# Two places for the normalised probabilities, and two cast operands that change slots, in a hybrid attention and pooling layer

## The chip, the cores and the metric

The kernel runs on one core of a Trainium2 chip. The metric is the device time of one execution in microseconds (us), the median over several runs; less is better.

The core's engines work in parallel, each through its own queue in order: PE multiplies matrices (PEld loads its weights), DVE and POOL work elementwise, ACT does the same and the functions (exp, sigmoid, square), SP issues the DMAs. They wait for each other by semaphores. PE writes its results into PSUM banks; everything else here lies in SBUF.

## The reference

x is 4096 tokens of 1024 channels, float32. One layer:

```python
h = rmsnorm(x, pre_norm_g)
q, k, v, g_a, u_p, g_p = split(h @ w_in)          # 512, 128, 128, 512, 512, 512 columns
# attention: 8 query heads, 2 key/value heads of 64; |i - j| <= 128, blocks of 128 queries
s = where(valid, q @ k.T * scale + bias, -1e30)
m = maximum(max(s), sink)
p = exp(s - m) / (sum(exp(s - m)) + exp(sink - m))
a = (p @ v) * silu(g_a)
# pooling: centred means over 2, 4, 8, 16 tokens minus the token, a linear map, a scale
b = multiscale_pool(u_p, pool_w, pool_scale) * silu(g_p)
x = x + rmsnorm(concat([a, b]) @ w_out, post_norm_g)
```

## The kernel before

Float32 accuracy comes from pairs of float16 numbers: a value is split into a high part (a cast) and a low part (the value minus its cast), and a product is three float16 matmuls. A first phase makes the weights and, for all tokens, the gates g_a and the gated pooling result, which go to DRAM (`ga_scr`, `yp_scr`). It ends at about 555 us of the profile and the change doesn't touch it.

The second phase goes through the 32 blocks of 128 queries from block 31 down to block 0; one block is one slot. Blocks 2u and 2u + 1 form pair u (16 pairs). Each slot has two *halves* of four heads each; a half b, half goes through these steps:

- `scores` (PE, L650), `logits` (DVE, four custom instructions, L671: bias, mask and minimum), `exps` (ACT, L682, four; the sink enters by a column that POOL copies into the tile p, L665), `denominators` (DVE, L689 and L692: `den`, `rd`);
- `probs` (ACT, L704, four): p times rd as float16 into the first half of the tile `pn`; `rests` (DVE, L712, four): the low part into the second half of `pn`;
- `turn` (SP, L721): one transposing DMA from `pn` to `pt`; then `values` (PE, L792) for both halves of a block, and `gate` (DVE, L800).

`pn` has one place (`PN_BUFS = 1`), so the `probs` of a half wait until the transposing DMA of the half before has read it.

The output projection of a pair takes seven products instead of eight, by sums of its four quarters (Strassen's scheme in Winograd's form). Its left operands are y11 and y12, y22, and the four sums s1 to s4. Here a11 is the gated attention of block 2u + 1, a21 that of block 2u, and a12 and a22 are the pooling results of the two blocks, which `pool_in` loads (tiles yf1, yf0). Each operand is cast by `high` (ACT, L809) and completed by `low` (POOL, L813); `pair(t, u, name, f)` enters both. `sum1`, `sum3`, `sum2` (DVE, L842 to L848) and `sum4` (POOL, L851) form the sums. `product` (PE, L873) runs 12 matmuls; in the profile the products of y11, y12 and y22 write `m`, those of s1 to s4 write `ms`. `add` and `gain11` (DVE, L905, L893), `begin` and `square` (ACT, L883, L888), `gain` (POOL, L900), `mean` (DVE L915, POOL L920: `rs`), `residual` (DVE, L924) and `store` finish the pair in the tiles `mo`.

The product of s4 (`mix_p3`) is summed by PE onto the bank in which the product of s1 (`mix_p5`) lies, but one `add` needs the product of s1 alone; so s4 waits for this `add`.

In the steady part PE's order is, in an even slot: scores of half 0, the first q projection, values of the odd block above, scores of half 1, the second q projection, s3 (`mix_p7`), s1 (`mix_p5`). In the next odd slot: scores of half 0, s4 (`mix_p3`), the k and v projections, values of the even block above, scores of half 1, y11, y22, y12, s2 (`mix_p1`, `mix_p4`, `mix_p2`, `mix_p6`).

What sets the order on each engine is a list of due times: `due(t, fn, ...)` enters a call, `now[0]` is the planned time of PE, t0 its value at the start of a slot, and at the end the list is run in order of t. These times are a plan only; on the chip each engine runs its rows in the order that results, each as soon as its waits allow.

Of the kernel before, what the change touches and what calls it, by code (L numbers as in the profile page):

```python
# [9 lines left out]
F16 = mybir.dt.float16  # L10
# [7 lines left out]
P = 128  # L18
# [5 lines left out]
NB = S // P  # L24
BPM = T // P
NH = 8
PT_BUFS = 3
PN_BUFS = 1
EPS = 1e-6
NEG = -1e30  # L30

# [33 lines left out]
def hybrid_layer(ctx: ExitStack, tc, io, out):  # L65
# [76 lines left out]
    with ExitStack() as actx:  # L142
# [387 lines left out]
        for m in range(NM):  # L530
# [5 lines left out]
            for j in range(4):  # L536
                u = pa.tile([P, T + 16], F32, name=f"u{m}_{j}", tag="u", bufs=6)
# [44 lines left out]
    pb = ctx.enter_context(tc.tile_pool(name="pb", bufs=2, reuse_waits="tile"))  # L582
# [19 lines left out]
    def split(dst_h, dst_l, acc):  # L602
        nc.scalar.mul(dst_h, acc, QKV_EVAC)
        nc.vector.scalar_tensor_tensor(
            out=dst_l, in0=acc, scalar=QKV_EVAC, in1=dst_h, op0=ALU.mult, op1=ALU.subtract
        )
# [22 lines left out]
    def due(t, fn, *args):  # L629
        plan.append((t, len(plan), fn, args))  # L630
# [67 lines left out]
    def probs(b, half, i):  # L698
        nk = len(keys(b)) * P
        if i == 0:  # L700
            pn_t[b, half] = pb.tile(
                [P, 2 * 4 * 3 * P], F16, name=f"pn{b}_{half}", tag="pn", bufs=PN_BUFS
            )
# [52 lines left out]
        split(k_all[:, 0, ts], k_all[:, 1, ts], kv_t[u][:, 0])  # L756

    def keep_v(u):
        v = pb.tile([P, 2, 2, P], F16, name=f"vv{u}", tag="v", bufs=4)
        split(v[:, 0], v[:, 1], kv_t.pop(u)[:, 1].rearrange("p (b d) -> p b d", b=2))  # L760
        v_t[u] = v

# [41 lines left out]
    at, yf, y_t, mo_t, z_t, ss_t, xr_t, rs_t = {}, {}, {}, {}, {}, {}, {}, {}  # L804

    def high(u, name, f):

        y_t[u, name] = pb.tile([P, 4, 2, P], F16, name=f"y{name}_{u}", tag=f"y{name}", bufs=1)
        nc.scalar.copy(y_t[u, name][:, :, 0], f(u))  # L809

    def low(u, name, f):
# [3 lines left out]
    def pair(t, u, name, f):  # L815
        due(t, high, u, name, f)
        due(t + 0.65, low, u, name, f)
# [35 lines left out]
    def sums(u, t):  # L853
        due(t, sum1, u)
        due(t + 0.05, sum3, u)
        due(t + 0.1, sum2, u)
        pair(t + 1.4, u, "s2", a11)
        pair(t + (10.0 if u > 1 else 2.0 + 2.0 * u), u, "s3", a21)
        pair(t + (10.6 if u > 1 else 2.6 + 2.0 * u), u, "s1", a_s1)
        due(t + 5.0, sum4, u)  # L860
        pair(t + (11.3 if u > 1 else 7.0), u, "s4", a12)

    LO, HI = slice(0, 512), slice(512, D)
# [76 lines left out]
    now = [0.0]  # L940
    dummy = pb1.tile([P, 1], F32, name="dummy")

    def pe(us, fn, *args):

        due(now[0], fn, *args)
        now[0] += us
        return now[0]
# [4 lines left out]
    def visit(b, half):  # L952
        now[0] = max(now[0], free[0])
        t = max(pe(1.1, scores, b, half), free[1])
        softmax(b, half, t)
        free[:] = t + 2.9, t + 7.9

    def do_kv(u, i=2, late=0.0):
        pe(2.6, proj_k, u, i)
        t = pe(2.8, proj_v, u)  # L960
        due(t + late, keep_k, u)
        due(t + late + 0.5, keep_v, u)

    def do_q(u, half, late=0.0):
        due(pe(5.3, proj_q, u, half) - half + late, keep_q, u, half)

    def attend(b):
        t = pe(2.1, values, b)
        due(t, gate, b)
        if b % 2:  # L970
            pair(t + 0.8, b // 2, "11", a11)
        else:
            sums(b // 2, t + 0.7)
# [3 lines left out]
    def mix_p1(u):  # L977
        due(pe(M, product, u, "11", O11, 0) - 2.0, begin, u)

    def mix_p4(u):  # L980
        pe(M, product, u, "22", OT4, 2)

    def mix_p2(u):
        t = pe(M, product, u, "12", O21, 0, True)
        due(t, square, u, 0, 0, 0)
        due(t + 0.1, gain11, u)

    def mix_p6(u):
        due(pe(M, product, u, "s2", OT2, 1), add, u, (0, HI), (0, HI), 1)

    def mix_p7(u):
        t = pe(M, product, u, "s3", OT3, 0)
        due(t - 1.5, add, u, (1, HI), (0, HI), 0)
        due(t - 1.4, add, u, (1, LO), (1, HI), 2)
        due(t + 1.4, square, u, 1, 0)
        due(t + 2.0, gain, u, 1, LO)

    def mix_p5(u):
        t = pe(M, product, u, "s1", OT1, 1)
        due(t, add, u, (1, HI), (1, HI), 1)  # L1000
        due(t + 0.7, square, u, 1, 1)
        due(t + 1.4, gain, u, 1, HI)
        finish(u, 1, t + (1.5 if u == 0 else 4.0))

    def mix_p3(u):
        t = pe(M, product, u, "s4", O22, 1, True)
        due(t, add, u, (0, HI), (0, HI), 1)
        due(t + 0.7, square, u, 0, 1)
        due(t + 1.4, gain, u, 0, HI)
        finish(u, 0, t + (1.5 if u == 0 else 4.0))  # L1010

    def finish(u, i, t):

        due(t, mean, u, i)
        for n, cs in enumerate((LO, HI) if u == 0 else (slice(0, D),)):
            due(t + 2.0 + 0.7 * n, residual, u, i, cs)
            due(t + 3.4 + 0.7 * n, store, u, i, cs)
# [3 lines left out]
    u = NU - 1  # L1021
# [10 lines left out]
    for b in reversed(range(NB)):  # L1032
        u = b // 2
        t0 = now[0]
        due(t0 + 10.0, load_ga, b)
        if b % 2 == 0 and 0 < b < NB - 2:
            due(t0 + 9.0, load_xr, u + 1, 1)
            due(t0 + 9.0, load_xr, u + 1, 0)
        if b > 0:
            visit(b, 0)  # L1040
        if b == NB - 1:
            do_q(u, 1, 2.8)
            due(now[0] + 0.1, load_x, u - 2)
            now[0] += 2.5
            visit(b, 1)
            do_kv(u - 1, 2, 2.5)
            now[0] += 3.0
        elif b == NB - 3:
            due(free[1], load_wo, OT3)
            mix_p4(u + 1)  # L1050
            mix_p1(u + 1)
            attend(b + 1)
            visit(b, 1)
            due(free[1], load_wo, OT1)
            due(free[1] + 8.0, load_wo, O22)
            do_kv(u - 1, 1)
            mix_p2(u + 1)
            mix_p6(u + 1)
        elif b == 1:
            mix_p3(u + 2)  # L1060
            mix_p4(u + 1)
            visit(b, 1)
            attend(b + 1)
            mix_p1(u + 1)
            mix_p2(u + 1)
            visit(b - 1, 0)
            mix_p6(u + 1)
        elif b % 2:
            mix_p3(u + 2)
            do_kv(u - 1)  # L1070
            attend(b + 1)
            visit(b, 1)
            mix_p1(u + 1)
            mix_p4(u + 1)
            mix_p2(u + 1)
            mix_p6(u + 1)
        elif b:
            do_q(u - 1, 0, 2.0 * (b == NB - 2))
            if b < NB - 2:
                attend(b + 1)  # L1080
            visit(b, 1)
            do_q(u - 1, 1, 2.0 * (b == NB - 2))
            due(now[0] + 2.1, load_x, u - 3)
            if b == NB - 2:
                attend(b + 1)
            else:
                mix_p7(u + 1)
                mix_p5(u + 1)
        else:
            due(t0, load_xr, 1, 1)  # L1090
            due(t0, load_xr, 1, 0)
            mix_p7(1)
            visit(b, 1)
            mix_p5(1)
            attend(1)
            mix_p3(1)
            mix_p4(0)
            mix_p1(0)
            attend(0)
            due(now[0] + 1.0, load_xr, 0, 1)  # L1100
            due(now[0] + 1.0, load_xr, 0, 0)
            mix_p2(0)
            now[0] += 3.0
            mix_p6(0)
            mix_p7(0)
            mix_p5(0)
            mix_p3(0)
        if b % 2 and b < NB - 1:
            due(now[0] - 1.0, pool_in, u, 0)
            due(now[0] + 2.0, pool_in, u, 1)  # L1110
        elif b % 2 == 0:
            t = t0 + 8.6 + 5.0 * (b == NB - 2)
            pair(t, u, "22", a22)
            pair(t + 0.4, u, "12", a12)
    E = mybir.EngineType
    with tc.manual_schedule(engines={E.PE, E.DVE, E.Activation, E.Pool, E.SP}):
        for t, n, fn, args in sorted(plan, key=lambda s: s[:2]):
# [73 lines left out]
```

## Time and profile before

| | us |
|---|---|
| median of 3 runs (lowest, highest) | 1285.51 (1284.38, 1286.82) |
| the profiled execution | 1288.93 |
| its span in the profile | 1287.2 |
| PE busy, in all | 1214.8 |
| DVE busy | 823.8 |
| ACT busy | 637.3 |
| POOL busy | 344.9 |

The span is the time from the first instruction to the last; the profiled execution took 1.7 us more. Busy time is that in which an engine works on an instruction; waiting is not busy. In the rows of the trace a name stands without its number, so `pn` is any half's tile; in the order of instructions below, pn16_1 is the tile of block 16, half 1, and y22_8 the operand y22 of pair 8 (the number behind the last underscore only tells tiles apart).

### The profile page before, as it was taken

How to read it: one execution, taken by the hardware profiler on the slowest of the kernel's cores; microseconds unless marked ns; L12 is line 12 of the kernel's file. 1: busy time of each engine (PE TensorE's matmuls, PEld its weight loads, DVE VectorE, ACT ScalarE, POOL GpSimd, SP SyncE). 2: the span in 40 equal slices, each digit the busy share in tenths (PEclk: the TensorE clock that was granted, in tenths of full speed). 3: DMA queues.
4: the chain of work that ended last, by engine and by line, in shares of the span. 5: the costliest groups of instructions: out<-in, count | busy, mean ns of one | idle time of the engine just before them, and what ended most of it. 6: DMA issues, size and time to landing. Idle time of an engine off the chain costs nothing. (4 is left out here: it accounts for less than half of the span.)

```text
span 1287.2 us, 22201 instructions
## 1 busy us (share of the span) xinstructions
PE 1214.8 (94%) x8630; PEld 703.9 (55%) x8632; DVE 823.8 (64%) x1717; ACT 637.3 (50%) x1352; POOL 344.9 (27%) x356
## 2 busy tenths in 40 slices
PE   5998999999999989989999999999999999999975
PEld 3643444444444434466675766666666757665632
DVE  4576263717155744436777777877787777778774
ACT  5365241512164521135755666566556656666651
POOL 2022020201020101101343333343334433333442
PEclk9998999999999999999999999999999999999998
DMA  7659485827159731275957765776676577656663
GB/s 228 229 144 286 161 207 154 244 92 229 33 173 272 225 106 42 63 232 124 274 118 189 186 169 140 188 181 137 183 187 167 116 184 193 169 136 156 148 147 115
DMA packets 337754, 216.49 MB, mean 168 GB/s; under 512 B 266944, under 2 KB 308544, under 8 KB 334064
## 3 DMA queue, kind: packets, MB, share of 16 engines
q1 hardware_dynamic: 337648, 215.07, 62.3%
q8 instruction: 67, 1.10, 0.4%
q14 instruction: 39, 0.32, 0.1%
HBM read 93.38 MB, written 56.13 MB: 116 GB/s over the span
## 5 line engine op out<-in xcount | busy, mean ns | idle before, releaser
L132 PEld LDWEIGHTS <-wa_h 128*128 128x128 f16 x1520 | 149.3, 98 | 186.2 <-issue 10.1
L712 DVE SCALAR_TENSOR_TENSOR pn<-p,rd,pn 128x384 f16<-128x384 f32 (+1 forms) x256 | 166.5, 696 | 55.3 <-ACT pn L704 55.1
L873 PE MATMUL ms<-wo,ys 128*128 128x512 f16 x768 | 173.9, 379 | 23.3 <-DVE mo L905 19.6
L682 ACT ACTIVATE p<-p,nm 128x385 f32<-128x385 f32 (+1 forms) x256 | 153.1, 600 | 60.5 <-POOL p L665 43.6
L614 PE MATMUL aq<-xt,wb_h 128*128 128x256 f16 x1024 | 174.7, 274 | 0.0
L704 ACT ACTIVATE pn<-p,rd 128x384 f16<-128x384 f32 (+1 forms) x256 | 136.9, 597 | 67.1 <-DMA pt<-pn 44.4
L132 PE MATMUL u<-xt,wa_h 128*128 128x512 f16 x512 | 155.7, 382 | 6.1 <-DVE xp L181 5.5
L671 DVE CUSTOM_DVE_ANT_0 p<-s,bias,nsink 128x384 f32<-128x384 f32 (+1 forms) x256 | 156.0, 663 | 1.0 <-PE s L650 1.0
L132 PE MATMUL ga<-xt,wa_h 128*128 128x512 f16 x512 | 153.6, 379 | 0.0
L132 PE MATMUL gp<-xt,wa_h 128*128 128x512 f16 x496 | 150.3, 382 | 3.3 <-DVE s_gp L432 3.3
L614 PE MATMUL aq<-xt,wb_l 128*128 128x256 f16 x512 | 140.3, 274 | 0.0
L614 PEld LDWEIGHTS <-wb_h 128*128 128x128 f16 x1280 | 125.7, 98 | 25.5 <-issue 9.4
L873 PEld LDWEIGHTS <-ys 128*128 128x128 f16 x768 | 74.5, 98 | 112.4 <-issue 25.4
L873 PE MATMUL m<-wo,y 128*128 128x512 f16 x576 | 129.8, 383 | 1.7 <-POOL y L813 0.9
L132 PEld LDWEIGHTS <-wa_l 128*128 128x128 f16 x760 | 74.7, 98 | 94.0 <-issue 6.1
L900 POOL TENSOR_TENSOR mo<-mo,gpost 128x512 f32<-128x512 f32 x45 | 73.6, 1636 | 119.1 <-ACT jkb L888 117.7
L132 PE MATMUL u<-xt,wa_l 128*128 128x512 f16 x256 | 97.8, 382 | 0.1
L132 PE MATMUL ga<-xt,wa_l 128*128 128x512 f16 x256 | 97.0, 379 | 0.1
L464 POOL TENSOR_TENSOR yt<-yt,s_gp 128x512 f32<-128x512 f32 x32 | 46.6, 1456 | 185.9 <-DVE yt L460 86.6
L873 PEld LDWEIGHTS <-y 128*128 128x128 f16 x576 | 55.2, 98 | 72.2 <-issue 7.6
L132 PE MATMUL gp<-xt,wa_l 128*128 128x512 f16 x248 | 94.7, 382 | 0.0
L432 DVE SCALAR_TENSOR_TENSOR s_ga<-ga,s_ga 128x512 f32<-128x512 f32 x32 | 22.1, 689 | 93.9 <-ACT s_ga L431 93.9
(135 smaller groups left out, 1764.7 us busy)
## 6 DMA issues: line engine op xcount, KB each, us to landing
xn<-in_x SPq DMA_DIRECT2D x32, 512.0 KB, 6.0
xr<-in_x SPq DMA_DIRECT2D x32, 512.0 KB, 4.2
out<-xr SPq DMA_DIRECT2D x30, 512.0 KB, 3.8
x_scr<-xt SPq DMA_DIRECT2D x7, 2048.0 KB, 10.3
xt<-x_scr SPq DMA_DIRECT2D x14, 1024.0 KB, 7.3
ga_scr<-s_ga SPq DMA_DIRECT2D x32, 256.0 KB, 2.3
yp_scr<-yt SPq DMA_DIRECT2D x32, 256.0 KB, 2.7
yf<-yp_scr SPq DMA_DIRECT2D x32, 256.0 KB, 2.8
```

What stands on the lines that cost most here:

```text
L132: mm = nc.tensor.matmul(a3, w[:, k, :], x[:, :, kk, :], start=(n == 0), stop=(n == 3 * KT - 1))
L432: nc.vector.scalar_tensor_tensor(out=s, in0=acc, scalar=scale, in1=s, op0=ALU.mult, op1=ALU.mult)
L464: nc.gpsimd.tensor_tensor(out=t, in0=t, in1=sg, op=ALU.mult)
L614: nc.tensor.matmul(a3, w[:, j, k, :], x[:, :, kk, :], start=(n == 0), stop=(n == 3 * KT - 1))
L671: nc.vector.tensor_tensor_reduce(out=p_t[b, half][:, hh, :nk], in0=s_t[b, half][jj][:, gg, :nk], in1=bias[:, h, lo : lo + nk], scale=negc[ ...
L682: nc.scalar.activation(p[:, hh, : nk + 1], p[:, hh, : nk + 1], AF.Exp, bias=nm_t[b, half][:, hh : hh + 1], scale=-1.0, accum_out=den_t[b, ...
L704: nc.scalar.activation(prob_view(b, half)[:, 0, i], p_t[b, half][:, i, :nk], AF.Copy, scale=rd_t[b, half][:, i : i + 1],)
L712: nc.vector.scalar_tensor_tensor(out=pn4[:, 1, i], in0=p_t[b, half][:, i, :nk], scalar=rd_t[b, half][:, i : i + 1], in1=pn4[:, 0, i], op0= ...
L873: nc.tensor.matmul(z_t[u, tag], y[:, k, yi, :], wo[o][:, wi, k, :], start=(n == 0 and acc is None), stop=(n == 3 * HK - 1), skip_group_che ...
L900: eng.tensor_tensor(out=mo, in0=mo, in1=gpost[:, cs], op=ALU.mult)
```

## The change

`pn` gets a second place, so that the tiles of successive halves lie in turn in the one and the other. In the same edit the tile `v` goes from four places to three, and two operands lose places of their own: y12 lies in turn with s1 in one place, y22 with s3. The casts and subtractions of y22 and y12 are entered one slot later, in the odd slot in which their products run, instead of the even slot before. In `mix_p7` two of the three `add`s are entered half a microsecond of the plan earlier.

```diff
-PN_BUFS = 1
+PN_BUFS = 2
...
     def keep_v(u):
-        v = pb.tile([P, 2, 2, P], F16, name=f"vv{u}", tag="v", bufs=4)
+        v = pb.tile([P, 2, 2, P], F16, name=f"vv{u}", tag="v", bufs=3)
...
     def high(u, name, f):
-        y_t[u, name] = pb.tile([P, 4, 2, P], F16, name=f"y{name}_{u}", tag=f"y{name}", bufs=1)
+        tag = {"12": "s1", "22": "s3"}.get(name, name)
+        y_t[u, name] = pb.tile([P, 4, 2, P], F16, name=f"y{name}_{u}", tag=f"y{tag}", bufs=1)
...
     def mix_p7(u):
-        due(t - 1.5, add, u, (1, HI), (0, HI), 0)
-        due(t - 1.4, add, u, (1, LO), (1, HI), 2)
+        due(t - 2.0, add, u, (1, HI), (0, HI), 0)
+        due(t - 1.9, add, u, (1, LO), (1, HI), 2)
...
             mix_p5(1)
+            pair(now[0], 0, "22", a22)
+            pair(now[0] + 0.4, 0, "12", a12)
             attend(1)
...
-        elif b % 2 == 0:
-            t = t0 + 8.6 + 5.0 * (b == NB - 2)
-            pair(t, u, "22", a22)
-            pair(t + 0.4, u, "12", a12)
+        if b % 2 and 1 < b < NB - 3:
+            pair(t0 + 8.1, u + 1, "22", a22)
+            pair(t0 + 8.7, u + 1, "12", a12)
+        elif b == NB - 2:
+            pair(t0 + 13.6, u, "22", a22)
+            pair(t0 + 14.0, u, "12", a12)
+        elif b == 1:
+            pair(t0 + 0.1, 1, "22", a22)
+            pair(t0 + 0.5, 1, "12", a12)
```

Three places show what moves; PE's and SP's rows stand in the order of before.

DVE in slot 16, half 1, from `rd` to the first logits of slot 15 (pn16_1 the rests, mo9 the `add`s of pair 9, whose products ms3, m22 and ms1 are those of s3, y22 and s1). Before:

```order
L692 RECIPROCAL rd16_1_9005<-den16_1_9004 128x4
L604 SCALAR_TENSOR_TENSOR q7_1_9021<-aq7_1_8953,q7_1_9021 128x512
L712 SCALAR_TENSOR_TENSOR pn16_1_9024<-p16_1_9006,rd16_1_9005,pn16_1_9024 128x384 x3
L905 TENSOR_TENSOR mo9_1_8691<-ms3_9_9028,mo9_0_8690 128x512
L905 TENSOR_TENSOR mo9_1_8691<-m22_9_8703,mo9_1_8691 128x512
L712 SCALAR_TENSOR_TENSOR pn16_1_9024<-p16_1_9006,rd16_1_9005,pn16_1_9024 128x384
L905 TENSOR_TENSOR mo9_1_8691<-ms1_9_9051,mo9_1_8691 128x512
```

and now:

```order
L692 RECIPROCAL rd16_1_8999<-den16_1_8998 128x4
L604 SCALAR_TENSOR_TENSOR q7_1_9015<-aq7_1_8948,q7_1_9015 128x512
L712 SCALAR_TENSOR_TENSOR pn16_1_9018<-p16_1_9000,rd16_1_8999,pn16_1_9018 128x384 x2
L906 TENSOR_TENSOR mo9_1_8691<-ms3_9_9022,mo9_0_8690 128x512
L906 TENSOR_TENSOR mo9_1_8691<-m22_9_8703,mo9_1_8691 128x512
L712 SCALAR_TENSOR_TENSOR pn16_1_9018<-p16_1_9000,rd16_1_8999,pn16_1_9018 128x384 x2
L906 TENSOR_TENSOR mo9_1_8691<-ms1_9_9045,mo9_1_8691 128x512
```

The `add`s of s3 and y22 stand behind two rests instead of three.

POOL in slot 15, from the last `gain` of pair 9 to the sum of pair 8 (p15_1 is the copy of the sink into p). Before:

```order
L900 TENSOR_TENSOR mo9_0_8690<-mo9_0_8690,gpost_4376 128x512
L920 TENSOR_TENSOR rs9_0_9217<-ms9_0_9215,mhalf_70 128x1
L665 COPY p15_1_9316<-nsink_80 128x4
L813 TENSOR_TENSOR ys2_8_9325<-at17_8912,ys2_8_9325 128x4x128
L851 TENSOR_TENSOR yf1_8_8854<-yf1_8_8854,at17_8912 128x512
```

and now:

```order
L901 TENSOR_TENSOR mo9_0_8690<-mo9_0_8690,gpost_4376 128x512
L921 TENSOR_TENSOR rs9_0_9211<-ms9_0_9209,mhalf_70 128x1
L814 TENSOR_TENSOR y22_8_9214<-yf0_8_8759,y22_8_9214 128x4x128
L814 TENSOR_TENSOR y12_8_9216<-yf1_8_8854,y12_8_9216 128x4x128
L665 COPY p15_1_9316<-nsink_80 128x4
L814 TENSOR_TENSOR ys2_8_9325<-at17_8912,ys2_8_9325 128x4x128
L852 TENSOR_TENSOR yf1_8_8854<-yf1_8_8854,at17_8912 128x512
```

The subtractions of y22 and y12 of pair 8 came in slot 16 ahead of the copy into p16_1; they now stand between `rs` and the copy into p15_1. On ACT the two casts now stand right behind the four `probs` of block 15, half 0, ahead of the `k_all` cast.

POOL at the start of slot 1 (pairs 2 and 1). Before:

```order
L813 TENSOR_TENSOR y11_1_13089<-at3_13062,y11_1_13089 128x4x128
L900 TENSOR_TENSOR mo2_1_12853<-mo2_1_12853,gpost_4376 128x512
L665 COPY p1_0_13236<-nsink_80 128x4
L900 TENSOR_TENSOR mo2_1_12853<-mo2_1_12853,gpost_4376 128x512
L920 TENSOR_TENSOR rs2_1_13262<-ms2_1_13260,mhalf_70 128x1
```

and now:

```order
L901 TENSOR_TENSOR mo2_1_12853<-mo2_1_12853,gpost_4376 128x512
L814 TENSOR_TENSOR y22_1_13213<-yf0_1_12921,y22_1_13213 128x4x128
L814 TENSOR_TENSOR y12_1_13215<-yf1_1_13004,y12_1_13215 128x4x128
L665 COPY p1_0_13236<-nsink_80 128x4
L901 TENSOR_TENSOR mo2_1_12853<-mo2_1_12853,gpost_4376 128x512
L921 TENSOR_TENSOR rs2_1_13262<-ms2_1_13260,mhalf_70 128x1
```

Here the two subtractions of pair 1 come ahead of the copy into p1_0. In slot 0 those of pair 0, and their casts, come ahead of the last `exps` instead of between them, and one `add` comes ahead of the last logits of block 0, half 0.

## The prediction

> **What bounds the kernel now.** I read the stretches first, because the second phase (blocks 31 down to 0, from about 560 us) is where every changed line lies. Columns: stretch, its length, then busy time of PE, PEld, DVE, ACT, POOL, the granted clock, the DMA share, GB/s.
>
> ```profile
> 560.00:640.00 80.00, 71.00 (x662) 50.49 (x663) 51.64 (x134) 47.97 (x122) 15.26 (x18) 0.98 0.72 183
> 640.00:1200.00 560.00, 545.14 (x4890) 363.90 (x4890) 426.81 (x953) 346.19 (x865) 208.15 (x217) 1.00 0.66 165
> 1200.00:1288.00 88.00, 64.09 (x406) 32.25 (x400) 58.64 (x118) 39.13 (x101) 34.14 (x33) 0.93 0.53 135
> ```
>
> PE is the bound: in the middle stretch it idles 14.9 us of 560, in the start 9.0, in the end 23.9. No instruction count changes, so only this idle time can be won. The waits say what it is: first two rows of 640 to 1200, then two of 1200 to 1288 (total, times, longest).
>
> ```profile
> PE ms L873 <- DVE mo L905: 14.9, 12, 1.7
> ACT pn L704 <- DMA pt<-pn: 32.4, 25, 2.1
> ...
> PE ms L873 <- DVE mo L905: 4.7, 3, 2.1
> PE o L792 <- DMA pt<-pn: 4.7, 1, 4.7
> ```
>
> In the steady stretch all of PE's idle time is one wait, once for each two blocks, twelve times: a product waits for an `add` on DVE. ACT's wait for the transposing DMA (25 times) is the one that the second `pn` buffer removes. Are they one chain? One instance, PE, ACT and DVE in turn (start, length, what, and in brackets idle time before it and its releaser):
>
> ```profile
> 896.89 5.34 PE L873 MATMUL ms<-wo,ys 128*128 128x512 f16 x24
> 902.16 1.16 PE L650 MATMUL s<-k_all,q 64*128 64x256 f16 x24
> 904.30 2.75 PE L873 MATMUL ms<-wo,ys 128*128 128x512 f16 x12 [0.97 <-DVE mo L905]
> ...
> 897.55 0.58 ACT L603 ACTIVATE q<-aq 128x512 f16<-128x512 f32 x1
> 899.47 2.13 ACT L704 ACTIVATE pn<-p,rd 128x384 f16<-128x384 f32 x4 [1.34 <-DMA pt<-pn]
> ...
> 897.89 0.18 DVE L692 RECIPROCAL rd<-den 128x4 f32<-128x4 f32 x1
> 898.16 0.69 DVE L604 SCALAR_TENSOR_TENSOR q<-aq,q 128x512 f16<-128x512 f32 x1
> 900.12 1.68 DVE L712 SCALAR_TENSOR_TENSOR pn<-p,rd,pn 128x384 f16<-128x384 f32 x3 [1.26 <-ACT pn L704]
> 901.71 0.68 DVE L905 TENSOR_TENSOR mo<-ms,mo 128x512 f32<-128x512 f32 x1
> 902.43 0.69 DVE L905 TENSOR_TENSOR mo<-m,mo 128x512 f32<-128x512 f32 x1
> 903.04 0.61 DVE L712 SCALAR_TENSOR_TENSOR pn<-p,rd,pn 128x384 f16<-128x384 f32 x1
> 903.56 0.68 DVE L905 TENSOR_TENSOR mo<-ms,mo 128x512 f32<-128x512 f32 x1
> ```
>
> They are. The products s3 and s1 end at 902.23 (896.89 + 5.34), scores follow to 903.32, and s4, which sums onto the bank of s1, may start only when the last `add` has read that bank, at 904.24. That `add` is 1.33 us behind the end of s1 because DVE began its four rests at 900.12, held by ACT's first `probs` at 899.47, held 1.34 us by the transpose of the half before.
>
> **The change, part by part.**
>
> *Second `pn` buffer, steady stretch.* `rd` is there at 898.07, ACT's q cast ends at 898.13, so `probs` start at 898.15 and the first is done after about 0.6. DVE is free of its q at 898.85 and starts the rests there instead of 900.12: 1.27 earlier. Four rests and two `add`s took 900.12 to 903.56, 3.44 us, so the last `add` could start at 902.29. Its input, s1, ends at 902.23. It runs 902.3 to 903.0, and scores end at 903.3: the wait is gone with 0.3 to spare. Twelve of them: -14.9. Bounds: 0 if something else holds the `add`, -14.9 at most, since PE has no other idle time there. I take the whole.
>
> *The two `add`s one rest earlier.* Same instructions, same total on DVE; s3 is half of the 5.34 us and ends at 899.56, before two rests that start at 898.85 are through (two of 0.56, 899.97). So no stall is added: 0. If s3 were later, the stall would be at most 0.56 and the 0.3 of cover would be gone: +0.3 a pair at worst.
>
> *Casts of y22 and y12, one slot later.* They leave the even slot and come, on ACT, between the four `probs` of the next odd slot and the `k_all` cast; on POOL behind the second `rs`:
>
> ```profile
> 909.30 2.14 ACT L704 ACTIVATE pn<-p,rd 128x384 f16<-128x384 f32 x4 [0.70 <-DMA pt<-pn]
> 912.39 0.38 ACT L603 ACTIVATE k_all<-kv 128x256 f16<-128x256 f32 x1 [0.95 <-PE kv L748]
> 891.56 1.12 ACT L809 CAST y<-yf 128x512 f16<-128x512 f32 x2
> ...
> 912.78 0.86 POOL L920 TENSOR_TENSOR rs<-ms,mhalf 128x1 f32<-128x1 f32 x1 [1.74 <-DVE ms L915]
> 892.24 2.63 POOL L813 TENSOR_TENSOR y<-yf,y 128x512 f16<-128x512 f32 x2 [6.24 <-ACT y L809]
> ...
> 891.28 2.57 DVE L712 SCALAR_TENSOR_TENSOR pn<-p,rd,pn 128x384 f16<-128x384 f32 x3
> 914.35 1.27 DVE L924 SCALAR_TENSOR_TENSOR xr<-mo,rs,xr 128x1024 f32<-128x1024 f32 x1
> 917.71 0.69 DVE L848 TENSOR_TENSOR at<-s,at 128x512 f32<-128x512 f32 x1
> ```
>
> On ACT the two casts, 1.12 together, fit into the 0.95 of idle time ahead of `k_all` plus the 0.70 of DMA wait that ends: 0. If both were still in front of PE's `k_all`, the most they could cost is 1.12 a pair on a cast that PE needs only a slot later. On POOL they matter through DVE. Three rests beside y22's and y12's subtractions took 2.57 us, without them 1.68 (at 900.12): 0.89 lost to POOL. In their new place the subtractions start when `rs` ends, 913.64, and stand beside DVE's `residual` (914.35), `gate` and the three sums that end at 918.40, all ahead of the next logits. If each engine waits for the other's running instruction, y22 (half of 2.63) ends near 914.9, `residual` near 916.0, y12 near 917.2, and the sums start 0.4 to 0.9 late. Bounds: -0.89 a pair (the even slot is freed, and nothing is lost) to +2.63 (both go ahead of DVE). I take 0.4, nearest the alternation seen in the 2.57.
>
> [...]
>
> What is late then: logits, exps, `probs`, rests and the transpose of half 1, for which PE's `values` of the odd block wait. Its rows, one pair earlier (SP, then the landing of all 51 such DMAs from 640 to 1200 as min/median/max, then PE):
>
> ```profile
> 882.11 4.19 SPq L721 DMA_TRANSPOSE pt<-pn  x1
> DMA to landing us min/median/max: 5.4/5.5/6.5
> ...
> 888.45 2.16 PE L792 MATMUL o<-pt,vv 128*64 128x256 f16 x36
> ```
>
> Landed at 887.61 by the median, used at 888.45: 0.84 of slack, none at 6.5. Of 0.4 lateness most pairs see nothing, slow DMAs cost up to 0.4; I take 0.1 a pair, +1.3 in all (bounds 0 and 12 x 2.63 = 31).
>
> *Shared places, and `v` with three buffers.* y22's place was last read by s3 of the pair before, y12's by s1, over at 902.23, and the casts come after 909. `v` is reused after the `values` at 888.45, over 15 us ahead of the next projection, which stands behind 904.30 in PE's queue. SP's order is unchanged; its transposes only issue earlier. All 0, with that cover; if a place were late, the cast would wait behind a product of 2.6 us (half of 5.34), at most once a pair.
>
> *Start.* Here the wait for the buffer is longest:
>
> ```profile
> 571.27 0.49 ACT L682 ACTIVATE p<-p,nm 128x257 f32<-128x257 f32 x1
> 576.53 1.70 ACT L704 ACTIVATE pn<-p,rd 128x256 f16<-128x256 f32 x4 [4.67 <-DMA pt<-pn]
> 578.14 0.36 ACT L603 ACTIVATE k_all<-kv 128x256 f16<-128x256 f32 x1
> ...
> 578.55 1.51 PE L650 MATMUL s<-k_all,q 64*128 64x384 f16 x12 [3.73 <-ACT k_all L603]
> ```
>
> ACT's idle 4.67 began at 571.86; two short DVE steps like the `rd` of 0.18 above come before `probs`, so these can start near 572.4. They take 1.70, the `k_all` cast then lies at 574.1 to 574.5, and PE was ready at 574.82 (578.55 - 3.73): -3.7, all of it (bounds 0 and -3.7).
>
> *End.* In slot 1 the two subtractions of pair 1 come ahead of POOL's copy into `p`, which exps wait for; in slot 0 `probs` lose their wait:
>
> ```profile
> 1214.71 0.19 POOL L665 COPY p<-nsink 128x4 f32<-128x4 f32 x1
> 1214.94 0.62 ACT L682 ACTIVATE p<-p,nm 128x385 f32<-128x385 f32 x1 [0.33 <-POOL p L665]
> ...
> 1241.03 0.18 DVE L692 RECIPROCAL rd<-den 128x4 f32<-128x4 f32 x1
> 1242.80 0.91 ACT L704 ACTIVATE pn<-p,rd 128x256 f16<-128x256 f32 x2 [2.56 <-DMA pt<-pn]
> ...
> 1256.58 1.85 SPq L721 DMA_TRANSPOSE pt<-pn  x1
> ```
>
> Slot 1 holds a thirteenth wait of the steady kind, about 1.6 (4.7 / 3). With it gone the chain comes to that copy 1.6 us earlier and then meets subtractions of up to 2.63 ahead of it: I count the gain of this wait as eaten, 0. At 1242.80 `probs` could start at 1241.2, 1.6 earlier; an `add` put ahead of the last logits takes 0.6 back; the two casts that stood between the last exps (1.12 together, as above) now stand ahead of them, where ACT waits for DVE anyhow, and give some 0.7 back. The transpose at 1256.58, for which PE then waits 4.7, comes about 1.7 earlier, and all behind it: -1.7 (bounds +1 and -4.7, the three waits there).
>
> Sum: -14.9 + 1.3 - 3.7 - 1.7 = **-19.0**. The profiled execution took 1288.93 (span 1287.2, and 1.7 around it that stays), so it would take 1269.9. It lies 3.4 above the median of the runs, 1285.5, and the rows tell of differences, not of that offset: 1285.5 - 19.0 = **1266.5**.
>
> **The rivals.**
> *B, half given back.* The sums are 0.9 late or more and slow DMAs are common: 0.7 a pair instead of 0.1 at the `values`, 8 in all; 1273. For it: the slack of 0.84 is thin. Against: the even slot wins 0.89 back each pair.
> *C, slower.* Both subtractions run ahead of DVE's sums, the odd `values` start up to 2.63 late and lose 1.8 to 2.6 of it (slack 0.84 to 0): 12 x 2.2 = 26 against 20.3 won, about 1291. It decides from 20.3 / 12 = 1.7 a pair. Against: in the 2.57 one rest got in between the two.
> *D, the `add` is held by something else* (DVE full, a place not free): the DMA wait goes, PE's stays; only start and end win, or not even these: 1280 to 1286.
>
> **How the numbers follow.** A (1259 to 1272, bounds of the end and of the lock) 0.73; B 0.13; D 0.07; C 0.07. From 1259 to 1277 lie A and more than half of B, 0.81. 0.2% is 2.6 us, about the spread of the runs before (1284.4 to 1286.8), and less can't be told from none: faster A, B and some of D, 0.88; same 0.05; slower 0.07.
>
> **What would show it.** Right: no wait of `probs` for the transposing DMA between 640 and 1200; PE's wait for `mo` there near 0; PE not idle for `k_all` at the start; the first three rests of an even slot in 1.7 instead of 2.57; the transpose at the end about 20 us ahead of 1256.58. The lock: `residual` or the first sum behind a POOL subtraction in odd slots, and a new row of PE `o` waiting for `pt`, about 1 us in all. Wrong: that row above 8 us, or PE still waiting for `mo` with `probs` early.

## The result, and the profile after

The changed kernel takes 1266.55 us (median of 4 runs, 1263.15 to 1269.67) against 1284.95 for the kernel before beside it: ratio 0.9855, 95% interval 0.9826 to 0.9884. The profiled execution took 1267.33, its span 1265.5.

The stretches again, with the columns of before (length, busy PE, PEld, DVE, ACT, POOL, granted clock, DMA share, GB/s), the last one up to the new end:

```profile
560.00:640.00 80.00, 75.35 (x724) 54.60 (x723) 56.76 (x147) 52.66 (x136) 17.52 (x20) 1.00 0.76 190
640.00:1200.00 560.00, 559.72 (x4987) 370.93 (x4985) 440.28 (x979) 353.84 (x885) 229.71 (x224) 1.00 0.67 168
1200.00:1266.00 66.00, 43.04 (x237) 19.36 (x234) 40.66 (x78) 25.03 (x65) 24.55 (x24) 0.90 0.49 128
```

In the middle PE went from 545.14 us busy of 560 to 559.72. The view lists waits above 0.15 us; of PE's, one row is left there, and it names another pair of instructions than before:

```profile
PE aq L614 <- DVE mo L894: 0.3, 1, 0.3
```

The same instance as in the prediction (slot 16; PE, ACT, DVE):

```profile
883.70 5.34 PE L874 MATMUL ms<-wo,ys 128*128 128x512 f16 x24
888.97 1.16 PE L650 MATMUL s<-k_all,q 64*128 64x256 f16 x24
890.07 2.12 PE L874 MATMUL ms<-wo,ys 128*128 128x512 f16 x9
...
884.47 2.13 ACT L704 ACTIVATE pn<-p,rd 128x384 f16<-128x384 f32 x4
...
884.21 0.18 DVE L692 RECIPROCAL rd<-den 128x4 f32<-128x4 f32 x1
...
885.13 1.14 DVE L712 SCALAR_TENSOR_TENSOR pn<-p,rd,pn 128x384 f16<-128x384 f32 x2
886.49 0.69 DVE L906 TENSOR_TENSOR mo<-ms,mo 128x512 f32<-128x512 f32 x1 [0.22 <-PE ms L874]
887.21 0.69 DVE L906 TENSOR_TENSOR mo<-m,mo 128x512 f32<-128x512 f32 x1
887.82 1.14 DVE L712 SCALAR_TENSOR_TENSOR pn<-p,rd,pn 128x384 f16<-128x384 f32 x2
889.08 0.69 DVE L906 TENSOR_TENSOR mo<-ms,mo 128x512 f32<-128x512 f32 x1
```

`probs` start at 884.47, right behind `rd` (ends 884.39), with no wait for a DMA. The last `add` now ends at 889.77, scores at 890.13, and s4 follows without a gap.

Where the 21.6 us between the two profiled executions lie, from the starts of the same PE work in both traces:

| stretch of the profile | predicted | measured |
|---|---|---|
| first phase, to the first scores (560.48, now 558.58; unchanged code) | 0 | -1.9 |
| start, to the scores of block 30, half 1 (586.87, now 579.95) | -3.7 | -5.0 |
| steady, to the product s4 of pair 3 (1169.38, now 1147.67) | -14.9 + 1.3 | -14.8 |
| end, to the end of the span | -1.7 | +0.1 |
| second phase in all | -19.0 | -19.7 |

The first phase differs by as much from one profile of the same code to the next (first scores at 558.58 in this profile of the changed kernel, at 556.49 in another), so below the second phase is counted by itself. The end differs by 1.2 between profiles in which its code is the same (in "The end" below), so its +0.1 is 0 within that.

### The profile page after: what moved, and what is told of

It reads as the page before. It is cut to its first block, busy times and chain, and to the rows that moved or that the text cites. A ratio compares the mean times of both kernels' runs of the same rounds, so it can differ in the third digit from the quotient of the medians.

```text
span 1265.5 us, 22233 instructions
## 1 busy us (share of the span) xinstructions
PE 1213.4 (96%) x8630; PEld 702.9 (56%) x8632; DVE 824.8 (65%) x1717; ACT 636.0 (50%) x1352; POOL 360.2 (28%) x356
## 5 line engine op out<-in xcount | busy, mean ns | idle before, releaser
L712 DVE SCALAR_TENSOR_TENSOR pn<-p,rd,pn 128x384 f16<-128x384 f32 (+1 forms) x256 | 161.0, 674 | 24.7 <-ACT pn L704 24.7
```

The costliest lines, as they stand in the source:

```text
L712: nc.vector.scalar_tensor_tensor(out=pn4[:, 1, i], in0=p_t[b, half][:, i, :nk], scalar=rd_t[b, half][:, i : i + 1], in1=pn4[:, 0, i], op0= ...
```

## The experiments

**Is it the buffer, or the moved casts?** Two kernels with one part each.

```diff
 # from the changed kernel
-PN_BUFS = 2
+PN_BUFS = 1
```

> The changed kernel with one place for pn again; the moved casts, the shared places, v with three buffers and the earlier adds stay. Theory (the second pn place carries the gain, the moved casts only free DVE and POOL in the even slot): the probs of half 1 wait for the transposing DMA again, so PE waits for mo once a pair again; the wait is shorter than before, since the rests of the even slot keep their pitch of 0.53 (they won about 0.45 a pair): 12 x (1.24 - 0.45) = 9.5 in the steady stretch, and the start loses its 4 to 5 again. 1279 to 1283. Rival (the moved casts make the gain, the second place is idle): 1266, no wait of PE for mo in the steady stretch.

```diff
 # from the kernel before
-PT_BUFS = 3
-PN_BUFS = 1
+PT_BUFS = 2
+PN_BUFS = 2
```

> The kernel before with a second place for pn and nothing else of the change; for room in SBUF the tile pt goes from three places to two. Theory (the buffer alone carries the gain): the twelve waits of PE for mo and the wait for k_all at the start go, the rests beside the subtractions stay at 2.57 and nothing is late for it: 1264 to 1269. A place of pt that comes late could hold a transpose by up to 1.2 a pair, which the slack of the values should hide. Rival (the casts must leave the even slot too, because the rests of half 1 need it): a wait of PE for mo of 0.5 or more a pair stays, 1272 or more.

The moves without the buffer: 1283.85, ratio to before 0.9994 (0.9977 to 1.0012). The buffer without the moves: 1265.37, 0.9841 (0.9808 to 0.9874). The buffer alone carries the gain. Without it, the waits between 640 and 1180 (ACT, then PE) are these:

```profile
ACT pn L704 <- DMA pt<-pn: 32.6, 24, 2.0
...
PE ms L874 <- DVE mo L906: 8.4, 12, 1.2
PE aq L614 <- DVE mo L894: 4.3, 4, 1.4
```

ACT waits for the transpose as before (32.4 then), and PE for the `add` 0.70 a pair instead of 1.24: the casts that left the even slot gave 0.54 back there, 0.45 had been expected. But a second wait stands beside it, for L894 (`gain11`), up to 1.4 at a time. It will come back below.

With the buffer alone PE is busy without a gap, in the row of its stretch:

```profile
640.00:1180.00 540.00, 540.00 (x4856) 360.31 (x4855) 428.06 (x942) 341.32 (x853) 206.32 (x214) 1.00 0.68 170
```

At about 600 us PE has one wait of 4.2 for a transpose there (1.1 in the kernel before and in the changed one). That is probably the price of the place taken from `pt`, the only other edit of this kernel; no run takes the two apart.

Two lengths from PE's rows tell the parts apart better than single waits: the start, from the first scores to those of block 30, half 1, and 13 pairs of the steady part, from the scores of block 27, half 0, to those of block 1, half 0 (us).

| kernel | start | 13 pairs |
|---|---|---|
| before | 26.4 | 572.5 |
| moves without the buffer | 26.5 | 571.2 |
| buffer without the moves | 21.4 | 557.0 |
| changed | 21.4 | 557.9 |

The buffer alone gives the whole 5.0 of the start and 15.5 in the steady part; the moves beside it cost 0.9 there, about 0.05 a pair and 0.3 once.

**The two `add`s.**

```diff
-        due(t - 2.0, add, u, (1, HI), (0, HI), 0)
-        due(t - 1.9, add, u, (1, LO), (1, HI), 2)
+        due(t - 1.5, add, u, (1, HI), (0, HI), 0)
+        due(t - 1.4, add, u, (1, LO), (1, HI), 2)
```

> The changed kernel with the two adds of s3 and y22 back behind three rests. Theory (the adds' place is worth nothing, since the last add had 0.3 of cover): within 0.2% of the changed kernel, 1264 to 1269, at most 0.1 of wait for mo a pair. Rival (the early adds are what lets the last add be ready for s4): PE waits for mo 0.3 to 0.5 a pair again, 1270 to 1273.

1266.14, ratio 0.9845 (0.9826 to 0.9864), and no wait of PE for `mo` of L906 between 640 and 1180. In the steady part their place is worth nothing that can be measured.

**What POOL's subtractions cost DVE.** In the changed kernel, slot 15, first POOL, then DVE; the last row is the first sum in the kernel before:

```profile
899.38 3.25 POOL L814 TENSOR_TENSOR y<-yf,y 128x512 f16<-128x512 f32 x2
...
900.12 1.50 DVE L925 SCALAR_TENSOR_TENSOR xr<-mo,rs,xr 128x1024 f32<-128x1024 f32 x1
...
902.26 0.93 DVE L843 TENSOR_TENSOR s<-at,yf 128x512 f32<-128x512 f32 x1
903.22 0.69 DVE L846 TENSOR_TENSOR at<-at,at 128x512 f32<-128x512 f32 x1
903.95 0.69 DVE L849 TENSOR_TENSOR at<-s,at 128x512 f32<-128x512 f32 x1
```

```profile
916.26 0.69 DVE L842 TENSOR_TENSOR s<-at,yf 128x512 f32<-128x512 f32 x1
```

`residual` takes 1.50 instead of 1.27 and the first sum 0.93 instead of 0.69: 0.47 in all, against the 0.4 of the prediction. To see where such lateness begins to cost, POOL did each of these subtractions twice:

```diff
-        nc.gpsimd.tensor_tensor(out=y[:, :, 1], in0=f(u), in1=y[:, :, 0], op=ALU.subtract)
+        for _ in range(2 if name in ("22", "12") and 2 <= u < NU - 1 else 1):
+            nc.gpsimd.tensor_tensor(out=y[:, :, 1], in0=f(u), in1=y[:, :, 0], op=ALU.subtract)
```

> The changed kernel in which POOL does each subtraction of y22 and y12 twice, with the same values, for pairs 2 to 14. It takes the lock between DVE and POOL to where rivals B and C would have it. Theory (DVE is blocked for the running subtraction only and alternates, so the sums come about 0.45 late with one set and about 2.0 late with two; the values of the odd block have 0.46 of slack): a new wait of PE o for pt of about 1.1 a pair, 12 x 1.1 = 13, 1277 to 1282. Rival (DVE's delay does not grow, since only one subtraction is ever in its way): 1266, no such wait, and only the copy into p or the operand s2 late. Rival C's price (the whole extra time goes ahead of DVE, 2.1 to 2.6 late, all of it lost): 12 x 2.1 = 25, 1291.

1288.74, ratio 1.0022 (1.0005 to 1.0039): the whole gain is gone. Its DVE and POOL in the same slot, and the only wait of PE between 640 and 1180:

```profile
908.68 6.38 POOL L815 TENSOR_TENSOR y<-yf,y 128x512 f16<-128x512 f32 x4
...
911.55 0.93 DVE L844 TENSOR_TENSOR s<-at,yf 128x512 f32<-128x512 f32 x1
912.52 1.53 DVE L847 TENSOR_TENSOR at<-at,at 128x512 f32<-128x512 f32 x1
914.08 1.53 DVE L850 TENSOR_TENSOR at<-s,at 128x512 f32<-128x512 f32 x1
...
PE aq L614 <- DVE mo L895: 19.3, 12, 1.9
```

Each sum beside a subtraction now takes up to 0.84 more, and a subtraction 1.60 in the mean (6.38 for four) against 1.17 for that of y11 in the changed kernel. So both engines take longer side by side, as in the 2.57 of the prediction: there the third rest took 1.51 instead of 0.61, and the second subtraction, begun before that rest's end, 1.47. The sums end 1.68 later than in the changed kernel (5.07 instead of 3.39 behind the start of that slot's y11 product), and PE waits 1.59 in a typical pair; the 13 pairs take 579.7 instead of 557.9, 1.68 each. So the theory had the lateness right (0.47 + 1.68, about 2.1) and the place and the price wrong: not 1.1 at the `values`, but all of the 1.68, at the q projection, for `gain11`. The rows at that place (DVE, PE) show why, first in the changed kernel, then with the doubled subtractions:

```profile
912.10 0.68 DVE L894 TENSOR_TENSOR mo<-m,gpost 128x512 f32<-128x512 f32 x1
...
912.84 0.27 PE L614 MATMUL aq<-xt,wb_h 128*128 128x256 f16 x1
```

```profile
923.08 0.69 DVE L895 TENSOR_TENSOR mo<-m,gpost 128x512 f32<-128x512 f32 x1
...
923.82 0.27 PE L614 MATMUL aq<-xt,wb_h 128*128 128x256 f16 x1 [1.58 <-DVE mo L895]
```

`gain11` stands behind the four rests of the odd half 1 and frees the bank that the next q projection writes. In the changed kernel it ends at 912.78 and PE takes the bank at 912.84, 0.06 later. That is not slack, although two expectations below call it so: where PE waits 1.58 for `gain11` it starts just as far behind it (923.77 to 923.82, 0.05). It is the hand-over from one engine to the other, and the changed kernel has no slack left. In the kernel before there was 0.46, so about 0.41 free:

```profile
925.87 0.68 DVE L893 TENSOR_TENSOR mo<-m,gpost 128x512 f32<-128x512 f32 x1
...
927.01 0.28 PE L614 MATMUL aq<-xt,wb_h 128*128 128x256 f16 x1
```

The 0.47 that DVE loses beside the subtractions used up these 0.41 and cost the rest, the 0.05 a pair of the table.

**Is `gain11` the deadline?** The doubled subtractions again, with `gain11` ahead of these rests, where DVE idles 0.7. In a first form `gain11` stood ahead of the product of y12 too, took that of y11 alone, and the product waited for it:

```diff
-        due(t + 0.1, gain11, u)
+        due(t - 2.8, gain11, u)
```

> The kernel with the doubled subtractions, and in it gain11 of each pair ahead of the four rests of the odd half 1 instead of behind them (DVE idles 0.7 there). With the subtractions doubled PE lost 1.59 a pair, and its wait stood at the q projection, for gain11, not at the values, for pt. Theory (the odd slot has two deadlines for DVE's lateness: gain11, which frees the bank that the q projection takes, with about 0.06 of slack, and the turn for the values with 0.46): the wait for gain11 goes; what is left is the square on ACT, which reads the same bank (0.75 a pair) and then the values for pt (0.45), together 1.2 a pair: 12 to 13 pairs x 0.4 = 5 less than 1288.7, so 1283 to 1285. Rival (the q projection waits for something that is late with gain11, and it is only named by the profile): 1288.7, still 1.6 a pair. Rival (gain11 is the only deadline): 1266 to 1268.

1363.28, ratio 1.0595 (1.0568 to 1.0623). So this kernel leaves the product of y12 out of that quarter of the result, and it doesn't answer the question; but its twelve waits say something else (below). In the second form the product is entered 0.4 earlier, PE's order stays, and `gain11` reads the sum:

```diff
-        t = pe(M, product, u, "12", O21, 0, True)
+        t = now[0] = now[0] + M
+        due(t - M - 0.4, product, u, "12", O21, 0, True)
         due(t, square, u, 0, 0, 0)
-        due(t + 0.1, gain11, u)
+        due(t - 2.8, gain11, u)
```

> As the run before it of this kind, with the product of y12 entered ahead of gain11, so that gain11 reads its sum: the doubled subtractions, and gain11 ahead of the four rests of the odd half 1, where DVE idles 0.7. Theory (two deadlines in the odd slot: gain11, which frees the bank that the q projection takes, with 0.06 of slack, and the turn for the values with 0.46): the q projection then waits for the square on ACT (0.75 a pair) and the values for pt (0.45), 1.2 a pair together instead of 1.59: 1283 to 1285. Rival (gain11 is only named, something else is late): 1288.7, 1.6 a pair. Rival (gain11 is the only deadline): 1266 to 1268.

1284.45, ratio 0.9999 (0.9990 to 1.0008). That lies in the range of the theory only because two misses cancel: the steady part gave back more than expected, and the edit made a new wait in the last block (PE for `ys`, 4.2, some 5 us in all). In the steady part PE waited 0.84 in a typical pair instead of 1.59, all at the square, the next reader of that bank, and nothing at the `values`. Waits of PE, then the `values` of one odd block and the transpose of its half 1 with its landing time:

```profile
PE aq L614 <- ACT jkb L890: 10.3, 12, 1.1
```

```profile
L792 PE MATMUL o<-pt,vv x36: 272/273/297, 923.8 to 925.7; 128*64 128x256 f16 x36
```

```profile
L721 SPq DMA_TRANSPOSE pt<-pn x1: 3662/3662/3662, 918.6 to 918.6; - x1
...
DMA to landing us min/median/max: 5.5/5.5/5.5
```

That transpose landed at 924.1, 0.3 behind the first of the 36 `values` matmuls, and PE did not wait: the first 18, about 1.05 us (half of 2.1), read half 0 alone. The expected 0.45 a pair at the `values` is 0 for this reason.

**The end.** Where the thirteenth wait went shows in PE's scores. All times are counted from the scores of block 2, half 1 (us):

| kernel | block 1, half 0 | 1, 1 | 0, 0 | 0, 1 | last transpose | end |
|---|---|---|---|---|---|---|
| before | 11.61 | 19.61 | 29.06 | 38.61 | 57.07 | 87.64 |
| changed (two profiles) | 11.61 | 17.97 | 28.35 | 37.97 | 57.11, 57.76 | 87.66, 88.30 |
| buffer without moves | 11.61 | 17.97 | 27.43 | 36.98 | 54.59 | 84.75 |
| edit of the end | 11.61 | 18.98 | 29.25 | 38.28 | 56.22 | 87.14 |
| last cast of y12 alone | 11.61 | 17.98 | 28.35 | 37.96 | 55.52 | 86.45 |

The buffer alone wins 1.6 in slot 1 and ends 2.9 earlier; with the moves the 1.6 is there at 17.97 and gone by the last transpose. Single profiles of the same end differ: the start edit and the doubled subtractions, which leave the end's code as it is in the changed kernel, have their last transpose at 57.98 and 58.25 and end at 88.64 and 88.82, and the edit of the end in a second kernel has 57.45 and 88.39. Differences of up to about 1.2 in the last two columns are therefore not read; the scores before them agree within 0.02.

```diff
-            pair(now[0] + 0.4, 0, "12", a12)
+            pair(now[0] + 5.0, 0, "12", a12)
...
-            pair(t0 + 0.1, 1, "22", a22)
-            pair(t0 + 0.5, 1, "12", a12)
+            pair(t0 - 1.6, 1, "22", a22)
+            pair(t0 + 8.3, 1, "12", a12)
```

> The changed kernel; only at the end the casts and subtractions of pair 1 move: those of y22 1.7 of the plan earlier, those of y12 behind the copy into p1_0 (8 later), and those of y12 of pair 0 4.6 later, behind the last exps. Theory (what the buffer won at the end was given back by subtractions and casts that stand ahead of POOL's copy and of ACT's exps): exps(1,0) no longer wait 1.6 for POOL's copy, exps(0,1) are no longer behind a cast that waits for a load; together about -3: 1263 to 1264.5. Rival (the end is set by the chain of half 0 in cold rows, the casts only fill a wait): within 0.2% of the changed kernel, 1264.5 to 1269.

1266.43, ratio 0.9844 (0.9826 to 0.9863); the changed kernel once more, on the same chip: 1266.07, 0.9849 (0.9826 to 0.9872). No gain: slot 0 won 1.9 to the last transpose (0.7 in the second kernel with this edit), and slot 1 lost 1.0, where the subtraction of y22 and the `gain` behind it now ran beside the last rests of block 2, so that the `add` behind these, for which s4 waits, came 1.3 late. Taken apart, only the first line of the edit:

> The changed kernel with one edit: the cast of y12 of pair 0 behind the last exps, as before the change, instead of ahead of them, where it waits 3.5 for the load of yf1. In the edit of the end that moved both pairs, slot 0 won 1.6 to 1.8 from the first scores of half 1 of block 1 to the last transpose, and slot 1 lost 1.0. Theory (the end's gain was eaten in slot 0 by that cast): the last exps start 0.3 to 0.6 behind their logits instead of 2.7, the last transpose issues 1.4 to 1.8 earlier: 1264 to 1265. Rival (the transpose then lands no earlier, or another wait takes the time): 1266.

1264.75, ratio 0.9852 (0.9829 to 0.9874). The time can't tell it from the changed kernel; the rows can. The changed kernel (first logits of block 0, half 1; ACT; the last transpose), and then this one (ACT, SP):

```profile
1223.64 0.54 DVE L671 CUSTOM_DVE_ANT_0 p<-s,bias,nsink 128x256 f32<-128x256 f32 x1
...
1225.70 0.62 ACT L810 CAST y<-yf 128x512 f16<-128x512 f32 x1 [3.53 <-DMA yf<-yp_scr]
1226.85 0.50 ACT L682 ACTIVATE p<-p,nm 128x257 f32<-128x257 f32 x1
...
1234.97 1.89 SPq L721 DMA_TRANSPOSE pt<-pn  x1
```

```profile
1222.37 0.49 ACT L682 ACTIVATE p<-p,nm 128x257 f32<-128x257 f32 x1
...
1231.65 2.74 SPq L721 DMA_TRANSPOSE pt<-pn  x1
```

ACT sat 3.53 in front of the cast of y12 of pair 0, which waits for its load, with the logits ready behind it. Moved, the last exps come 2.8 earlier and the last transpose 1.6 (the two profiles lie 1.7 apart there; 55.52 against 57.11 in the table). Against the four profiles with the end as changed, the end wins 1.2 to 2.4. The buffer alone ends another 1.7 earlier (84.75). 0.9 of this lies between the scores of block 1, half 1, and those of block 0, half 0 (10.4 against 9.5 in the table), and the rows say what stands there: the two subtractions of pair 1, ahead of POOL's copy for which exps wait. The changed kernel, then the buffer alone:

```profile
1190.55 2.28 POOL L814 TENSOR_TENSOR y<-yf,y 128x512 f16<-128x512 f32 x2
...
1193.00 0.62 ACT L682 ACTIVATE p<-p,nm 128x385 f32<-128x385 f32 x1 [1.64 <-POOL p L665]
```

```profile
1194.19 0.62 ACT L682 ACTIVATE p<-p,nm 128x385 f32<-128x385 f32 x1 [0.33 <-POOL p L665]
```

Counted as in the table these exps start at 15.13 instead of 13.57. From the scores of block 0, half 0, to the last transpose both take 27.2. The other 0.8 lies behind the last transpose; these runs don't show its cause.

**The start.**

```diff
-            do_kv(u - 1, 1)
+            do_kv(u - 1, 1, -2.0)
...
-            pair(t0 + 14.0, u, "12", a12)
+            pair(t0 + 17.5, u, "12", a12)
```

> The changed kernel; only at the start the k_all and v casts of pair 14 are entered 2.0 earlier and those of y12 of pair 15 3.5 later. Theory: three waits of PE that are left between 560 and 640 go (1.1 for pt, 0.5 for k_all, 1.5 behind probs): about -3, 1263 to 1264.5. Rival (each of them only uncovers the next): -1 or less, 1265.5 or more.

> The changed kernel with both edits, that of the end and that of the start; they lie 500 us apart and should add: about -6, 1260 to 1262. Rival (the steady stretch eats a head start): no better than the better of the two.

> The changed kernel once more, beside the edits of it: 1264 to 1269 with a median near 1266.5; its profile's start and end within 0.5 of the other profile of it, if single profiles can be compared stretch by stretch.

The start alone: 1262.44, ratio 0.9819 (0.9796 to 0.9842); with the edit of the end 1262.43, 0.9821 (0.9800 to 0.9841), so that edit adds nothing here either. Of the three waits the one behind `probs` (1.5) went, that for `pt` fell from 1.1 to 0.8, that for `k_all` stayed. From the first scores to those of block 2, half 1, it is 617.0 instead of 619.3: -2.3, a little less than was expected. The control's start is within 0.1 of the first profile, its end within 0.7, beyond the 0.5 that was expected.

**All that helped, together:** the start, the last cast of y12, and in slot 1 y12's cast behind two `probs` (`t0 + 6.6` for `t0 + 0.5`).

> The edit of the start, that cast of y12 of pair 0, and in slot 1 the cast of y12 of pair 1 behind two probs of block 1, half 0, so that its subtraction stands neither ahead of the copy into p1_0 nor ahead of the second rs. Theory (the three are independent): start -2.3 to -3.5, slot 0 -1.6, slot 1 -0.5 to -1.1; 1260 to 1262. Rival (the end gives nothing): 1262.5 to 1263.5, the time of the edit of the start alone.

1260.85 (median of 6, 1259.78 to 1268.10), ratio 0.9811 (0.9798 to 0.9825), the lowest median of all these kernels; its interval overlaps that of the start alone. The start gave its 2.3 and slot 0 about 1 (the end at 86.82). Slot 1 gave nothing: its scores of block 0, half 0, came at 28.33 as against 28.35. Exps came 1.1 earlier there, but the subtraction of y12 now ran beside three rests of that half, which took 3.59 instead of 2.69.

## Why the prediction was right, point by point

The mechanism of the main term is shown, and it is most of the gain. That the median, 1266.55, lies within 0.1 of the 1266.5 foreseen is luck: the start gave 1.3 more than its term, the end 1.8 less, and the `values` nothing of their 1.3, while a wait that was not foreseen took 0.9.

**Second buffer, steady: -14.9, measured -15.5** in the 13 pairs with the buffer alone (-14.8 in the changed kernel, with what its moves cost); that is a little more than the waits that the view lists. Shown: the buffer alone removes all twelve waits. The chain was read rightly, down to the spare time: 0.3 was foreseen, 0.36 is in the rows (889.77 to 890.13).

**The `add`s: 0, measured 0.** The first now waits 0.22 for s3, inside the cover.

**The lock: 0.4, measured 0.47,** and it cost about 0.05 a pair (next point). The lock, the waiting of DVE and POOL for each other's running instruction, was the author's estimate from the 2.57; the rows show the times alone. In the changed kernel `residual` took 1.50 (1.27 before) and the first sum 0.93 (0.69), and beside doubled subtractions the next two sums took 1.53 (0.69).

**The wait of the odd `values`: +1.3, measured 0.** The step that failed is the slack of 0.84, counted to the first matmul of `values`. The tile that comes late is that of half 1, and half 0 is read for 1.05 us before it. The deadline that does bind was not in the prediction at all: `gain11`, whose bank the q projection takes. The 0.47 used up the 0.41 that were free there, and the 13 pairs lost 0.9 in all, 0.3 of it in one pair. So a cost near the +1.3 is there, but at another place and for another reason. Rival C's point of decision, 1.7 a pair, held in size: with the sums 2.1 late, the loss was 1.68 a pair and the kernel as slow as before. Its place and its slack were wrong. Rivals B and D did not come about, but C was nearer than its 0.07 looked: no slack was left, and what came later than that was lost whole, as the 1.68 were.

**The start: -3.7, measured -5.0,** beyond the bounds given, and all of it from the buffer (26.4 to 21.4 with the buffer alone). The term that failed is PE's work behind the wait, which the prediction took as unchanged; an error of opposite sign stood beside it. The cast of `k_all` was put at 574.1 as if it waited for ACT alone; its input comes from PE just before:

```profile
570.46 1.71 ACT L704 ACTIVATE pn<-p,rd 128x256 f16<-128x256 f32 x4 [0.51 <-DVE rd L692]
572.95 0.38 ACT L603 ACTIVATE k_all<-kv 128x256 f16<-128x256 f32 x1 [0.79 <-PE kv L748]
...
573.39 1.28 PE L650 MATMUL s<-k_all,q 64*128 64x384 f16 x12 [0.47 <-ACT k_all L603]
```

So 0.47 of the wait stays, and the wait itself gave 3.3. The rest is the clock. Windows of before behind its wait, then of after at the same q projection (granted clock third from the end):

```profile
579.90:582.00 2.10, 2.10 (x12) 1.45 (x11) 2.10 (x8) 1.35 (x5) 0.00 (x0) 0.50 1.07 205
582.00:584.00 2.00, 2.00 (x15) 1.55 (x14) 0.70 (x4) 1.50 (x5) 0.00 (x0) 0.71 0.25 47
```

```profile
574.60:579.90 5.30, 5.30 (x50) 4.62 (x48) 3.69 (x13) 4.05 (x12) 0.00 (x0) 1.00 0.49 116
```

Before, the projection ran at a clock of 0.50 for some 3 us and took 6.88; now it takes 5.35: another -1.5, and 0.2 in the scores ahead of it, which the wait's own row doesn't show.

**The end: -1.7, measured +0.1** (up to +1.2 in other profiles). The gain of the thirteenth wait was counted as eaten by the subtractions ahead of the copy; 0.6 of its 1.6 was still there at the scores of block 0, half 1 (37.97 instead of 38.61). What failed is the 0.7 that the two casts ahead of the last exps were to give back, since "ACT waits for DVE anyhow": one of them waits for a load itself, 3.53 long, and held the exps. With that cast moved back the end gives -1.2 (86.45 against 87.64).

## What to carry to other kernels

When an engine's work gets later, list every reader that frees something for the bound engine, banks as well as data, and count its slack to the instruction that needs it, not to the start of its group: here the slack seen was 0.84, the real ones 0.41 and about 1.5. Time between a release and the start behind it is slack only in so far as it is longer than where the engine is seen to wait, here 0.05. A cast whose input comes by DMA is no filler for an idle engine unless the load has landed: here it held ACT for 3.53. And a buffer that removes a wait should be tried by itself first: here it gave all of the gain, and the moves that came with it only found the room, and cost 0.9 in the steady part.

## What was not expected of the hardware

Long waits of PE cost more than themselves in two of the kernels. The 3.7 us wait of before cost 1.5 more in the projection behind it, where the clock was 0.50. In the kernel with the misplaced `gain11`, PE waited 5.0 in each pair, and a pair took about 7.2 longer (50.1 instead of 42.9). The wait, and then a stretch from each of two pairs, whose waits end at 707.37 and at 758.20 (granted clock third from the end):

```profile
PE m L875 <- DVE mo L895: 59.6, 12, 5.0
...
709.80:712.40 2.60, 2.60 (x7) 0.88 (x6) 0.00 (x0) 0.00 (x0) 0.00 (x0) 0.50 0.62 118
...
760.90:764.00 3.10, 3.10 (x16) 1.37 (x14) 0.00 (x0) 1.70 (x5) 0.42 (x1) 1.00 0.81 154
```

The twelve waits of up to 1.7 in the kernel before left the clock of their stretch at 1.00, and those of 1.9 in the kernel with doubled subtractions cost no more than themselves (1.6 a pair), with the clock at 1.00 from 640 to 1180. Behind the wait of 3.7 the clock was 1.00 again from 583.2 on, 4.7 us after its end; behind the waits of 5.0 it was so sooner in one pair (1.00 again 2.7 us behind the wait) and later in another (0.50 still 5 us behind it). Pairs of the two kinds take 49.3 and 50.2 to 50.8 us, against 42.9 in the changed kernel. The longest wait in full work that is seen to leave the clock at 1.00 is one of 2.3 in the same kernel, at 609 us:

```profile
606.74:609.06 2.32, 0.01 (x1) 0.00 (x0) 1.40 (x5) 1.82 (x7) 1.20 (x1) 1.00 0.92 231
609.00:612.50 3.50, 3.44 (x16) 1.56 (x16) 2.89 (x7) 2.94 (x9) 0.00 (x0) 1.00 0.75 295
```

In the first phase, whose code is the same in both kernels, a wait of 3.3 that ends at 459.35 (before) had 0.50 behind it from 460.3 to 463.6, and one of 2.6 that ends at 457.67 (changed kernel) had 0.50 from 457.3 to 460.6, from ahead of its end. At the end, where PE waits often, the clock fell after a wait of 1.8 too (changed kernel: PE busy 3.25 of the 6.15 us from 1212.00 to 1218.15, then 0.50 from 1218.4 to 1221.8), so the length of one wait alone doesn't decide it.
